# Three sets of turned heads instead of two in the attention of a two-layer diffusion trunk, and the next pair's maxima ahead of the present pair's values

## The chip, the cores and the metric

One core of one Trainium2 chip runs the whole step. The metric is device time in microseconds (us) of one execution. TensorE is called PE in the profile (its weight loads PEld), VectorE DVE, ScalarE ACT, GpSimd POOL; SP issues most DMAs.

## The reference

Two layers with shared structure work on 512 latent tokens and 128 context tokens of width 1024. Each layer is a mixer (a state-space scan, an attention and a gated position mixing side by side, one output projection) and then a gated feed-forward with a short convolution. The change lies in the attention alone, which for the latent tokens is

```python
s = jnp.einsum('bqhd,bkhd->bhqk', q_blk, k).astype(F32) * ATTN_SCALE   # 8 heads, 96 deep
w = jax.nn.softmax(s, axis=-1).astype(v.dtype)                         # 512 queries, 128 + 512 keys
return jnp.einsum('bhqk,bkhd->bqhd', w, v)                             # 64 values a head
```

## The kernel before, in words

The attention of a layer (function `attention`) works on 8 heads in four pairs, p = 0 to 3. Everything is float32; products that need it are made of three matmuls of a high and a low part (qh, ql, kh, kl).

For each head h:
- `turn(h)` (L1223) transposes queries and keys of the head on PE into PSUM (tiles qt and kt, L147) and writes the high parts with ACT (L1229, L1236) and the low parts with DVE (L1230, L1237) into one of **two sets** of tiles, set h % 2. A set is free again when `scores` of the head before in it is done.
- `maxima(h)` (L1241) multiplies each of four blocks of 128 queries with all 640 keys (tile mx, L1248) and takes the negated maximum of each query with DVE (L1250).
- `max_row(h)` (L1254) transposes the four columns of maxima (tile nmt) and copies them with ACT as row 96 into qh (L1259). The row of ones in kh then subtracts the maximum inside the score matmul. `scores(h)` can't begin before it.
- `scores(h)` (L1261) makes five tiles of 128 keys by 512 queries (L1267 to L1269, PSUM tiles s, two slots) and ACT takes the exponential into tiles P (L1271, ten buffers for the ten tiles of a pair).

For each pair, the generator `weighted` (L1275) has two steps: first the sums over the keys' tiles of P (DVE, L1280 and L1282, two buffers Ps) and the **values** (PE, tile o, L1287, both heads side by side); then the **denominators** (PE, L1292) and the copies out of PSUM to yB and S (ACT, `put`, L1208 and L1211).

After pairs 1 and 3 (every two pairs, b = 0 and 1) one DVE reciprocal of 128 x 512 denominators runs (L1427), which two matmuls spread over the partitions (tile rs, L1433 and L1434); yB is scaled by it (L1436) and squared into the sums of a later norm (`squares`, L1350, temporary msq in the pool yb).

In the same stretch PE, SP and ACT do work that has nothing to do with the attention: `fill` is the generator `mod_blocks` (L230), which makes the modulation vectors of the second half of the layer. One step loads 512 KB of w_mod (SP, L258, three buffers raw), multiplies them (PE, tile mod, L261), and after four steps copies (ACT, L267), transposes (PE, modt) and reduces (DVE, L240 to L247). `maxima` gives way after each block of queries, and the caller then takes one step of `fill`. In pair 3 (no next heads) `merge_ac` and the output projection of the two other mixers (L1406 and on, tile wo) run beside the attention.

PSUM tiles: qt, nmt, mod, modt and a few more share two slots (`pz`, L79); kt, mx, o and rs share two slots of two banks (`pb`, L82); s has two slots (`pa`).

What sets the order of the work: the program is written in the order of the Python calls, and when it is built, a planner with a time model of its own issues to each engine, step by step, the earliest written instruction that it takes to be ready and that has its buffers. The written order is thus a ranking; each engine then executes its list in order, and waits at an instruction whose input is late. The loop over the pairs before:

```python
out = weighted(p, [scores(2 * p), scores(2 * p + 1)])
for h in heads:          # 2p + 2 and 2p + 3
    turn(h)
next(out)                # sums and values
for h in heads:
    for _ in maxima(h):
        next(fill, None)
next(out)                # denominators, put
for h in heads:
    max_row(h)
```

Of the kernel before, what the change touches and what calls it, by code (L numbers as in the profile page):

```python
# [11 lines left out]
F32R = mybir.dt.float32r  # L12
# [26 lines left out]
def spans(lo, hi):  # L39
    out = []  # L40
    if lo < 512:
        out.append((lo, min(hi, 512), 0))
    if hi > CX:
        out.append((max(lo, CX), hi, 1))
    return out


class Trunk:
# [1142 lines left out]
    def attention(self, l, M, yb, at, es, qs, ks, Vt, yB, yA, yc, ssc, fill):  # L1191


        nc, V, A = self.nc, self.nc.vector, self.nc.scalar
# [4 lines left out]
        def t(s, sh, dt=F32, bufs=1, pool=at):  # L1199
            return pool.tile(list(sh), dt, name=self.uid(s), tag=s, bufs=bufs)  # L1200

        S = t("S", [128, 2, 640])
        qh, ql, kh, kl = ([t(f"{nm}{i}", [97, n], F32R) for i in range(2)]
                          for nm, n in (("qh", 512), ("ql", 512), ("kh", 640), ("kl", 640)))

        def put(p, ps, sums, n, c):

            A.copy(yB[:, p, c:c + n], ps[:, :n])  # L1208
            r = slice(p % 2 * 64, p % 2 * 64 + 64)
            o = c if c < 512 else 512  # L1210
            A.copy(S[r, p // 2, o:o + n], sums[r, :n])  # L1211

        def constant_rows(i):
            nc.gpsimd.memset(ql[i][96:97].bitcast(F32), 0.0)
            nc.gpsimd.memset(kl[i][96:97].bitcast(F32), 0.0)
            nc.gpsimd.memset(kh[i][96:97].bitcast(F32), 1.0)

        for i in range(2):
            constant_rows(i)

        nml = {}

        def turn(h):  # L1223

            i = h % 2
            ps = self.pz("qt")
            for tt in range(4):
                self.tr(ps[:96, tt * 128:(tt + 1) * 128], qs[:, tt, h, :])
            A.activation(qh[i][:96], ps[:96], AF.Copy, scale=qg)  # L1229
            V.scalar_tensor_tensor(ql[i][:96], ps[:96], qg, qh[i][:96].bitcast(F32),  # L1230
                                   op0=OP.mult, op1=OP.subtract)
            pb = self.pb("kt")
            for kt in range(5):
                self.tr(pb[:96, kt // 4, (kt % 4) * 128:(kt % 4) * 128 + 128], ks[:, kt, h, :])
            for o, a, b in ((0, 0, 512), (1, 512, 640)):
                A.activation(kh[i][:96, a:b], pb[:96, o, :b - a], AF.Copy, scale=kg)  # L1236
                V.scalar_tensor_tensor(kl[i][:96, a:b], pb[:96, o, :b - a], kg,  # L1237
                                       kh[i][:96, a:b].bitcast(F32),
                                       op0=OP.mult, op1=OP.subtract)

        def maxima(h):  # L1241

            i = h % 2
            nm = nml[i] = t("nml", [128, 4], bufs=2)
            for tt in range(4):
                pb = self.pb("mx")
                for o in range(2):
                    mm(pb[:, o, :320], qh[i][:96, tt * 128:(tt + 1) * 128],  # L1248
                       kh[i][:96, o * 320:(o + 1) * 320], start=True, stop=True)
                V.tensor_reduce(nm[:, tt:tt + 1], pb[:, :, :320], axis=AX.XY, op=OP.max,  # L1250
                                negate=True)
                yield

        def max_row(h):  # L1254
            nm = nml[h % 2]
            ps = self.pz("nmt")
            for tt in range(4):
                self.tr(ps[0:1, tt * 128:(tt + 1) * 128], nm[:, tt:tt + 1])
            A.copy(qh[h % 2][96:97], ps[0:1])  # L1259

        def scores(h):  # L1261
            i = h % 2
            Ps = []
            for kt in range(5):
                ps = self.pa("s")
                kc_ = slice(kt * 128, (kt + 1) * 128)
                mm(ps, kh[i][:, kc_], qh[i], start=True, stop=False)  # L1267
                mm(ps, kh[i][:, kc_], ql[i], start=False, stop=False)
                mm(ps, kl[i][:, kc_], qh[i], start=False, stop=True)  # L1269
                P = t("P", [128, 512], bufs=10, pool=at2)  # L1270
                A.activation(P, ps, AF.Exp, scale=SCALE)  # L1271
                Ps.append(P)
            return Ps

        def weighted(p, Ps):  # L1275

            ss = []
            for i in range(2):
                s = t("Ps", [128, 512], bufs=2, pool=at2)
                V.tensor_tensor(s, Ps[i][0], Ps[i][1], op=OP.add)  # L1280
                for kt in range(2, 5):
                    V.tensor_tensor(s, s, Ps[i][kt], op=OP.add)  # L1282
                ss.append(s)
            pb = self.pb("o")
            for kt in range(5):
                for i in range(2):
                    mm(pb[i * 64:(i + 1) * 64, 0], Vt[:, kt, 2 * p + i], Ps[i][kt],  # L1287
                       start=kt == 0, stop=kt == 4)
            yield
            for i in range(2):  # L1290
                r = (2 * p + i) % 4 * 32
                mm(pb[r:r + 32, 1], self.ones[:, :32], ss[i], start=True, stop=True)  # L1292
            put(p, pb[:, 0], pb[:, 1], 512, 0)
            yield


        with self.tc.tile_pool(name=f"actx{l}", bufs=1, side=self.sides[1]) as cx:
            qc, kc = t("qc", [104, 8, 128], pool=cx), t("kc", [104, 8, 128], pool=cx)
            nc.sync.dma_start(out=kc[96:104].rearrange("p h c -> p (h c)"), in_=self.I["k_onehot"])
            for src, dst, g in ((qs[:, 4], qc, qg), (ks[:, 5], kc, kg)):  # L1300
                for hb in range(2):
                    ps = self.pa("ctr")
# [5 lines left out]
            nm = t("nm", [128, 8], pool=cx)  # L1308
            for hb in range(2):
                ps = self.pa("cmx")  # L1310
                for i in range(4):
                    h = 4 * hb + i
# [4 lines left out]
            ps = self.pa("nmt")  # L1317
# [5 lines left out]
            Ps = []  # L1323
            for hb in range(2):
                ps = self.pa("cs")
                for i in range(4):
                    h = 4 * hb + i
                    mm(ps[:, i * 128:(i + 1) * 128], kc[:, h], qc[:, h], start=True, stop=True)
                P = t("Pc", [128, 512], bufs=2, pool=cx)
                A.activation(P, ps, AF.Exp, scale=SCALE)  # L1330
                Ps.append(P)
            for _ in nms[1]:
                next(fill, None)
            for hb, P in enumerate(Ps):
                max_row(hb)
                for p in range(2 * hb, 2 * hb + 2):
                    po = self.pb("co")
                    for i in range(2):
                        h = 2 * p + i
# [7 lines left out]
        at2 = es.enter_context(self.tc.tile_pool(name=f"at2{l}", bufs=1, side=self.sides[1]))  # L1347


        def squares(y, tiles, ac, first):  # L1350
            for a, b, _ in spans(0, NT):
                for i in tiles:
                    if first and i == tiles[0]:
                        A.activation(ac[:, a:b], y[:, i, a:b], AF.Square)
                    else:
                        s = t("msq", [128, 512], pool=yb)
                        A.activation(s[:, :b - a], y[:, i, a:b], AF.Square)
                        V.tensor_tensor(ac[:, a:b], ac[:, a:b], s[:, :b - a], op=OP.add)
# [48 lines left out]
        for p in range(4):  # L1407
            if p == 3:
                yh = M.tile([128, KT, NT], F32R, name=self.uid("yh"), tag="hh", bufs=1)
                yl = M.tile([128, KT, NT], F32R, name=self.uid("yl"), tag="hl", bufs=1)  # L1410
                merge_ac()
                projection = self.project_ac(l, yh, yl)
                next(projection)
            heads = (2 * p + 2, 2 * p + 3) if p < 3 else ()
            out = weighted(p, [scores(2 * p), scores(2 * p + 1)])
            for h in heads:
                turn(h)
            next(out)
            for h in heads:
                for _ in maxima(h):  # L1420
                    next(fill, None)
            next(out)
            for h in heads:
                max_row(h)
            if p % 2:
                b = p // 2
                V.reciprocal(S[:, b, 0:512], S[:, b, 0:512])  # L1427
                if b:
                    for _ in fill:
                        pass  # L1430
                for j in range(2):
                    pb = self.pb("rs")
                    mm(pb[:, 0], self.sel[:, j], S[:, b, 0:512], start=True, stop=True)  # L1433
                    mm(pb[:, 1, :128], self.sel[:, j], S[:, b, 512:640], start=True, stop=True)  # L1434
                    for a, e, c in spans(0, NT):
                        V.tensor_tensor(yB[:, 2 * b + j, a:e], yB[:, 2 * b + j, a:e],  # L1436
                                        pb[:, c, :e - a], op=OP.mult)
                squares(yB, [2 * b, 2 * b + 1], ac, b == 0)
        ps = stats(ac)
# [316 lines left out]
```

## Time and profile before

| | us |
|---|---|
| median of 3 runs (lowest, highest) | 1826.63 (1825.92, 1826.67) |
| the profiled execution | 1826.58 |
| its span, first to last instruction | 1824.8 |
| attention pairs in layer 0, first score to the last reciprocal's use | 272.9 to 394.2 of the span |
| the same in layer 1 | 1153.3 to 1271.5 of the span |

The profile is of one execution; the span leaves out 1.78 us around the first and last instruction. Times in the rows are counted from the span's start. A row of the timeline gives start, length, engine, line, operation and, in brackets, how long the engine stood idle before it and for what. A row of the waits gives the total, the number and the longest of one kind. A stretch (windows) gives per engine the busy time, and PEclk, the share of full speed that TensorE's clock was granted (1.00 is 2.4 GHz, 0.50 is 1.2 GHz).

### The profile page before, as it was taken

The page shows a single profiled execution, that of the slowest core. Times are in us where ns is not written, and L with a number is a line of the kernel's source. Part 1 is how long each engine was busy: PE and PEld are TensorE (multiplying, and loading weights), DVE is VectorE, ACT ScalarE, POOL GpSimd, SP SyncE. Part 2 cuts the span into 40 slices and gives each one's busy share as a digit, 9 for nine tenths or more (in the row PEclk, how much of TensorE's full clock was granted, in tenths as well). Part 3 has the DMA queues.
Part 4 walks back from the last instruction along what each step waited for, and adds up shares of the span by engine and source line. Part 5 has one row for each costly group of instructions (what it writes and reads, how often), then busy time and mean ns, then how long its engine had stood idle before and what let it go on. Part 6 is the DMA issues. An engine that isn't in the chain of part 4 may idle for free.

```text
span 1824.8 us, 28970 instructions
## 1 busy us (share of the span) xinstructions
PE 1694.3 (93%) x11248; PEld 1512.6 (83%) x11248; DVE 1156.8 (63%) x2421; ACT 679.8 (37%) x1210; POOL 312.8 (17%) x738
## 2 busy tenths in 40 slices
PE   5878889999989999999999888999989999999998
PEld 3767755468889999999999876455989999999998
DVE  6887875667674646556477568566786464555564
ACT  4334454433452414224244346343344232332241
POOL 2886200000086060540000120000000000000000
PEclk7889789899899999999999978999989999999999
DMA  9265453301443523234132633540223131331221
GB/s 281 84 174 148 124 162 123 110 15 56 129 137 118 170 56 116 59 94 116 35 90 67 164 105 107 167 133 1 70 70 93 36 104 47 93 92 36 82 82 58
DMA packets 217577, 182.48 MB, mean 100 GB/s; under 512 B 33438, under 2 KB 202204, under 8 KB 217440
## 3 DMA queue, kind: packets, MB, share of 16 engines
q1 hardware_dynamic: 194736, 154.33, 28.2%
q0 software_dynamic: 8272, 23.87, 4.4%
q10 hardware_dynamic: 14432, 2.44, 0.7%
q8 instruction: 89, 1.46, 0.3%
q14 instruction: 48, 0.39, 0.1%
HBM read 161.94 MB, written 18.64 MB: 99 GB/s over the span
## 4 chain that ended last, share of the span: by engine, by line
PE 75%; DVE 10%; DMA 7%; ACT 4%; POOL 2%; issue 2%; ACTq 1%; SPq 0%; DVEq 0%; POOLq 0%
PE up L141 11%; PE up L143 11%; PE up L142 11%; PE dn L142 6%; PE dn L141 6%; PE dn L143 6%; PE o L1287 3%; PE mod L261 2%; DMA raw<-w_mod 2%; PE wo L141 1%; PE wo L143 1%; PE wo L142 1%; DMA raw<-ffn_w_up 1%; PE s L1267 1%; PE win L141 1%
## 5 line engine op out<-in xcount | busy, mean ns | idle before, releaser
L141 PE MATMUL up<-hh,whi 128*128 128x322 f32 x1408 | 435.6, 315 | 8.8 <-ACT hh L357 7.9
L143 PE MATMUL up<-hh,wlo 128*128 128x322 f32 x1408 | 440.9, 314 | 1.1 <-DVE wlo L118 1.0
L142 PE MATMUL up<-hl,whi 128*128 128x322 f32 x1408 | 439.7, 313 | 1.6 <-DVE hl L358 1.5
L141 PEld LDWEIGHTS up<-hh,whi 128*128 128x128 f32 x1408 | 266.1, 191 | 14.3 <-ACT hh L357 7.2
L142 PEld LDWEIGHTS up<-hl,whi 128*128 128x128 f32 x1408 | 268.8, 191 | 2.6 <-DVE hl L358 2.6
L143 PEld LDWEIGHTS up<-hh,wlo 128*128 128x128 f32 x1408 | 267.9, 190 | 2.9 <-DVE wlo L118 1.9
L118 DVE TENSOR_TENSOR wlo<-raw,whi 128x1024 fp32r<-128x1024 f32 (+1 forms) x116 | 146.7, 1266 | 142.2 <-ACT whi L117 141.0
L142 PE MATMUL dn<-glo,dh 128*128 128x322 f32 (+1 forms) x704 | 218.5, 312 | 0.2 <-DVE glo L118 0.2
L143 PE MATMUL dn<-gh,dl 128*128 128x322 f32 (+1 forms) x704 | 217.9, 311 | 0.0
L141 PE MATMUL dn<-gh,dh 128*128 128x322 f32 (+1 forms) x704 | 209.4, 312 | 4.5 <-DVE xT L1501 2.9
L1501 DVE SCALAR_TENSOR_TENSOR xT<-dn,mod,xT 128x320 f32<-128x320 f32 (+2 forms) x288 | 112.2, 435 | 129.5 <-PE dn L143 129.3
L117 ACT CAST whi<-raw 128x1024 fp32r<-128x1024 f32 (+1 forms) x116 | 120.5, 1040 | 151.1 <-PE up L142 56.8
L1532 ACT ACTIVATE cv<-up,prm,cw 128x321 f32<-128x321 f32 x88 | 54.3, 619 | 252.5 <-PE up L143 252.3
L141 PEld LDWEIGHTS dn<-gh,dh 128*128 128x128 f32 x704 | 131.0, 190 | 5.3 <-DVE xT L1501 3.1
L142 PEld LDWEIGHTS dn<-glo,dh 128*128 128x128 f32 x704 | 133.2, 189 | 0.5 <-DVE glo L118 0.5
L143 PEld LDWEIGHTS dn<-gh,dl 128*128 128x128 f32 x704 | 133.5, 190 | 0.0
L1533 DVE SCALAR_TENSOR_TENSOR cv<-up,cw,cv 128x320 f32<-128x320 f32 x88 | 48.3, 549 | 67.5 <-ACT cv L1532 67.5
L261 PE MATMUL mod<-raw,sT 128*32 128x256 f32 x768 | 64.5, 431 | 27.1 <-DMA raw<-w_mod 24.8
L118 DVE TENSOR_TENSOR dl<-raw,dh 128x1024 fp32r<-128x1024 f32 x44 | 54.0, 1227 | 45.8 <-ACT dh L117 45.6
L117 ACT CAST dh<-raw 128x1024 fp32r<-128x1024 f32 x44 | 46.1, 1047 | 56.8 <-DMA raw<-ffn_w_down 50.1
L261 PEld LDWEIGHTS mod<-raw,sT 128*32 128x32 f32 x768 | 19.5, 114 | 57.5 <-DMA raw<-w_mod 29.2
L1250 DVE TENSOR_REDUCE nml<-mx 128x1 f32<-128x640 f32 x64 | 50.9, 820 | 24.0 <-PE mx L1248 23.7
(472 smaller groups left out, 3422.5 us busy)
## 6 DMA issues: line engine op xcount, KB each, us to landing
raw<-w_mod SPq DMA_DIRECT2D x96, 512.0 KB, 4.6
raw<-ffn_w_up SPq DMA_DIRECT2D x88, 512.0 KB, 4.1
raw<-ffn_w_down SPq DMA_DIRECT2D x44, 512.0 KB, 3.5
raw<-w_in SPq DMA_DIRECT2D x10, 512.0 KB, 5.7
we<-WEd POOLq DMA_DIRECT2D x8, 512.0 KB, 4.1
qt<-Qd POOLq DMA_DIRECT2D x8, 512.0 KB, 5.1
raw<-w_out SPq DMA_DIRECT2D x16, 256.0 KB, 5.1
raw<-w_out SPq DMA_DIRECT2D x8, 512.0 KB, 3.4
```

Source lines behind the costliest of these rows:

```text
L117: self.nc.scalar.copy(hi, raw)
L118: self.nc.vector.tensor_tensor(lo, raw, hi.bitcast(F32), op=OP.subtract)
L141: mm(ps, wh, xh, start=start, stop=False)
L142: mm(ps, wh, xl, start=False, stop=False)
L143: mm(ps, wl, xh, start=False, stop=stop)
L261: nc.tensor.matmul(ps[j * 32:j * 32 + 32, c0:c0 + 256], self.sT[:, k0 + j, :], rv[:, j, :], start=k0 == 0, stop=k0 == 4)
L1250: V.tensor_reduce(nm[:, tt:tt + 1], pb[:, :, :320], axis=AX.XY, op=OP.max, negate=True)
L1267: mm(ps, kh[i][:, kc_], qh[i], start=True, stop=False)
L1287: mm(pb[i * 64:(i + 1) * 64, 0], Vt[:, kt, 2 * p + i], Ps[i][kt], start=kt == 0, stop=kt == 4)
L1501: self.nc.vector.scalar_tensor_tensor(self.xT[:, m, a:b], po[:, a - lo:b - lo], self.modcol(l, gi, m, c), self.xT[:, m, a:b], op0=OP.mult, ...
L1532: A.activation(z[:, 0:321], po[:, 0:321], AF.Identity, bias=b, scale=c1)
L1533: V.scalar_tensor_tensor(z[:, 1:321], po[:, 0:320], c0, z[:, 1:321], op0=OP.mult, op1=OP.add)
```

## The change

All in `attention`. There are three sets of turned queries and keys (index h % 3, three nml buffers), so turning a head waits for the scores of the head three before. P has nine buffers instead of ten; of the two sums Ps, the second uses the tile msq of the pool yb, which `squares` uses too. In the loop, each next head is turned, its maxima are taken (with a step of fill each) and its max_row is made, one head after the other, all written ahead of the present pair's sums, values and denominators. The reciprocal of 128 x 512 becomes four of 128 x 128.

```diff
-        qh, ql, kh, kl = ([t(f"{nm}{i}", [97, n], F32R) for i in range(2)]
+        qh, ql, kh, kl = ([t(f"{nm}{i}", [97, n], F32R) for i in range(3)]
...
-        for i in range(2):
+        for i in range(3):
             constant_rows(i)
...
-            i = h % 2
+            i = h % 3
...
-            nm = nml[i] = t("nml", [128, 4], bufs=2)
+            nm = nml[i] = t("nml", [128, 4], bufs=3)
...
-                P = t("P", [128, 512], bufs=10, pool=at2)
+                P = t("P", [128, 512], bufs=9, pool=at2)
...
-                s = t("Ps", [128, 512], bufs=2, pool=at2)
+                s = t("msq", [128, 512], pool=yb) if i else t("Ps", [128, 512], pool=at2)
...
             out = weighted(p, [scores(2 * p), scores(2 * p + 1)])
             for h in heads:
                 turn(h)
-            next(out)
-            for h in heads:
                 for _ in maxima(h):
                     next(fill, None)
+                max_row(h)
             next(out)
-            for h in heads:
-                max_row(h)
+            next(out)
             if p % 2:
                 b = p // 2
-                V.reciprocal(S[:, b, 0:512], S[:, b, 0:512])
+                for c in range(0, 512, 128):
+                    V.reciprocal(S[:, b, c:c + 128], S[:, b, c:c + 128])
```

## Rows read from the trace of the kernel before

**Rows 1.** The page: busy engines of the whole span, and shares of the chain.
```profile
PE 1694.3 (93%) x11248; PEld 1512.6 (83%) x11248; DVE 1156.8 (63%) x2421; ACT 679.8 (37%) x1210; POOL 312.8 (17%) x738
...
PE 75%; DVE 10%; DMA 7%; ACT 4%; POOL 2%; issue 2%; ACTq 1%; SPq 0%; DVEq 0%; POOLq 0%
```

**Rows 2.** Stretches of layer 0's four pairs; cut also at the clock's fall and rise.
```profile
272.92:307.44 34.52, 32.15 (x210) 16.72 (x207) 18.27 (x42) 15.93 (x36) 0.00 (x0) 1.00 0.46 147
307.44:334.79 27.35, 24.64 (x157) 12.49 (x158) 16.47 (x25) 11.44 (x21) 0.00 (x0) 1.00 0.47 145
334.79:344.61 9.82, 9.61 (x29) 6.29 (x30) 6.74 (x9) 3.86 (x5) 0.00 (x0) 0.50 0.59 188
344.61:367.94 23.33, 22.11 (x101) 12.99 (x101) 16.13 (x29) 10.87 (x22) 0.24 (x2) 0.94 0.00 0
367.94:394.23 26.29, 24.34 (x108) 13.68 (x107) 15.64 (x24) 10.60 (x21) 0.00 (x0) 0.98 0.00 1
```

**Rows 3.** The same view of layer 1's low stretch of the clock.
```profile
1215.15:1222.66 7.51, 7.43 (x26) 5.35 (x27) 5.95 (x9) 3.86 (x5) 0.00 (x0) 0.55 0.54 164
```

**Rows 4.** Waits of PE in layer 0's attention: total, times, longest.
```profile
PE mod L261 <- DMA raw<-w_mod: 3.0, 2, 2.1
PE rs L1433 <- DVE S L1427: 1.5, 1, 1.5
PE s L1267 <- ACT qh L1259: 0.8, 3, 0.3
PE mod L261 <- DVE ql L1230: 0.8, 1, 0.8
PE mx L1248 <- DVE nml L1250: 0.7, 2, 0.5
PE mx L1248 <- ACT S L1211: 0.6, 1, 0.6
...
PE nmt L147 <- ACT modev L267: 0.3, 1, 0.3
```

**Rows 5.** Waits of PE in layer 1's attention.
```profile
PE mod L261 <- DMA raw<-w_mod: 4.1, 2, 3.1
...
PE s L1267 <- ACT qh L1259: 0.6, 2, 0.3
...
PE mx L1248 <- DVE nml L1250: 0.5, 1, 0.5
```

**Rows 6.** Timeline of layer 0 between the second and the third pair.
```profile
328.96 3.35 DVE L1427 RECIPROCAL S<-S 128x512 f32<-128x512 f32 x1 [0.27 <-ACT S L1211]
...
333.39 0.64 PE L261 MATMUL mod<-raw,sT 128*32 128x256 f32 x8 [2.13 <-DMA raw<-w_mod]
...
338.15 0.79 PE L1267 MATMUL s<-qh,kh 97*128 97x512 f32 x1 [0.21 <-ACT qh L1259]
```

**Rows 7.** Timeline of layer 1: waits of PE at the same turn and the next.
```profile
1213.76 0.64 PE L261 MATMUL mod<-raw,sT 128*32 128x256 f32 x8 [3.08 <-DMA raw<-w_mod]
...
1215.16 0.54 PE L147 MATMUL nmt<-ident,nml 128*1 128x128 f32 x2 [0.27 <-ACT modev L267]
...
1240.95 0.85 PE L1248 MATMUL mx<-kh,qh 96*128 96x320 f32 x4 [0.59 <-ACT S L1211]
```

**Rows 8.** The tile of the denominators: durations in ns, least, median, most.
```profile
L1346 DVE RECIPROCAL S<-S x4: 952/953/954, 277.1 to 1161.0; 128x128 f32<-128x128 f32 x4
L1427 DVE RECIPROCAL S<-S x4: 3352/3353/3353, 329.0 to 1268.1; 128x512 f32<-128x512 f32 x4
```

**Rows 9.** Timeline of layer 0's first pair: maxima of head 2, then the last values.
```profile
297.31 0.56 PE L1248 MATMUL mx<-kh,qh 96*128 96x320 f32 x2
...
297.81 1.07 PE L1287 MATMUL o<-P,Vt 128*64 128x512 f32 x2
```

**Rows 10.** POOL's timeline: the first of the six memsets of the sets' rows.
```profile
250.67 0.52 POOL L1214 MEMSET ql<- 1x512 f32 x1 [31.83 <-DVE yA L830]
```

**Rows 11.** DVE's group of the maxima in layer 0's attention.
```profile
L1250 DVE TENSOR_REDUCE nml<-mx 128x1 f32<-128x640 f32 x26 | 20.7, 821 | 8.5 <-PE mx L1248 8.3
```

More of the change, by code (lines that the diff above doesn't have):

```diff
@@ L1241, in maxima @@
         def maxima(h):
-            i = h % 2
-            nm = nml[i] = t("nml", [128, 4], bufs=2)
+            i = h % 3
+            nm = nml[i] = t("nml", [128, 4], bufs=3)
             for tt in range(4):
@@ L1254, in max_row @@
         def max_row(h):
-            nm = nml[h % 2]
+            nm = nml[h % 3]
             ps = self.pz("nmt")
@@ L1258, in max_row @@
                 self.tr(ps[0:1, tt * 128:(tt + 1) * 128], nm[:, tt:tt + 1])
-            A.copy(qh[h % 2][96:97], ps[0:1])
+            A.copy(qh[h % 3][96:97], ps[0:1])
         def scores(h):
-            i = h % 2
+            i = h % 3
             Ps = []
```

## The prediction

> **What bounds the kernel now.** The page first: PE is busy 93% of the span and carries 75% of the chain [rows 1]. A change that adds or removes no matmul can win only where PE stands still or runs at a lower clock, so I look for those two, and only in the attention, since nothing else is edited.
>
> The stretches [rows 2, 3] come next: in each pair PE's column nearly fills the stretch. Of layer 0's 121.31 us, PE is idle in 8.5 (121.31 less the five busy times, 112.85). PEclk shows the second loss: 0.50 for 9.82 us in layer 0, 0.55 for 7.51 us in layer 1, both at the turn from the second pair to the third. The work done there would have taken 9.82 x 0.50 = 4.9 us less and 7.51 x 0.45 = 3.4 us less at full clock.
>
> Then who ended PE's waits [rows 4, 5]. The largest are not the attention's own: PE stands at a fill matmul whose load of w_mod hasn't landed, 3.0 us in layer 0 and 4.1 in layer 1, in each layer one of about 1 us and a long one. The long ones, 2.13 and 3.08 us [rows 6, 7], end just before the low clock begins. The waits of the turn from pair to pair are small: scores for the row of maxima, maxima for a reduction, for a PSUM slot that `put` frees, max_row's transposes for a slot behind modev. They come to 0.8 + 0.7 + 0.6 + 0.3 = 2.4 us in layer 0 [rows 4] and 0.6 + 0.5 + 0.6 + 0.3 = 2.0 in layer 1 [rows 5, 7].
>
> At the turn itself [rows 6]: the reciprocal holds DVE for 3.35 us from 328.96 while maxima of heads 4 and 5 still stand behind it; PE waits for the load until 333.39; the first score of the third pair starts at 338.15, right after the row of maxima.
>
> **The change part by part.** I sum against the profiled execution, 1826.58 us (span 1824.8 and 1.78 around it), which is 0.05 under the median of the runs.
>
> *Third set, maxima and max_row ahead of the values.* Number and size of PE's, ACT's and DVE's instructions stay. What moves ahead, per pair: 18 transposes, 8 blocks of maxima with their reductions of 0.82 us [rows 11], 8 steps of fill with their loads on SP, matmuls, modev copies and reductions, and two max_rows. What falls behind: 8 sums on DVE, the values, the denominators, put. SP's queue holds the same loads in the same order; only w_out's loads, which come behind the fill, could move, and they share its three buffers. POOL's queue is not passed. The gain is that a row of maxima is ready while the values, which wait for nothing late, still fill PE, so the small waits of the turn (2.4 + 2.0 = 4.4 us) can go. Their bounds are 0 and 4.4; I take 4.4, because each of them is a wait for a step that would now stand several us earlier. Late next is DVE: the maxima alone are 8 x 0.82 = 6.6 us in a pair, and the sums, whose reading frees P, now stand behind them. DVE is busy 16.47 of 27.35 us in the second pair [rows 2], so it isn't the bound.
>
> *The long waits for the load and the low clock behind them.* They are no wait of the attention, but they fall where the order has nothing but maxima and fill left for PE. With values and next scores at hand, the order can put those in front of a fill matmul whose load is late. If a long wait shrinks to about its short neighbour (0.9 and 1.0: the totals less the longest), layer 0 gains 1.2 us and 4.9 of clock, layer 1 gains 2.1 and 3.4. Bounds: nothing, and all four, 11.6 us. I take one of the two layers: 6.1 or 5.5, 5.8 in the middle. The order is fixed when the kernel is built, by assumed landings, so I can't claim both; the row nearest to such a claim, the same place in both layers, shows the same wait with 1 us of spread.
>
> *Reciprocals in four.* One of 128 x 512 takes 3.353 us, one of 128 x 128 takes 0.953 [rows 8]: four take 3.81, 0.46 more. At the end of pair 3 PE waits 1.5 us for it in each layer [rows 4], so it lies on the path there: 2 x 0.46 = +0.9. The matmul that uses it reads all 512 columns, so no piece lets it start earlier. After pair 1 the pieces let DVE slip other work between them; the maxima are then already ahead, so I count nothing. If that cover is gone, 0.9 more.
>
> *Nine P, one sum in msq.* The tenth exponential of a pair waits until the sum and the values have read the first tile, and behind it in ACT's queue stand copies of the next heads. One fewer buffer can't gain anything. At most it adds one values matmul out of turn, 1.07 us [rows 9], in each of 8 pairs: 8.6. The second sum of pair 2 also waits for the squares of pairs 0 and 1, behind the pieces of the reciprocal, and the P tiles it reads are held so long; pair 3's scores need them only after the merge. I take 0 for both, since PE has other work for 24.64 of 27.35 us in the second pair [rows 2], and keep 8.6 for the upper end.
>
> *Third set of constant rows.* Three more memsets on POOL, an estimate of 1.7 us from the 0.52 of the 512-wide one [rows 10] and two somewhat longer. Needed only by head 2, which is written behind the first scores at 272.92 [rows 2], 22 us later, and POOL idled 31.83 us before them. That wait is for a neighbour's memory; the larger sets reach further into it, which could hold the first turn back by something; nothing taken, 1.7 us if the cover is gone.
>
> Sum: -4.4 - 5.8 + 0.9 = -9.3, so 1817.3. With both layers' waits gone it is -4.4 - 11.6 + 0.9 = -15.1, so 1811.5.
>
> One reading speaks against this. A fill matmul in layer 0 waited 0.8 us for DVE's ql [rows 4], which is the reader of a qt tile: both share the two PSUM slots `pz`, and these stay two. The Trainium skill, Perfetto Trace Analysis, section Optimization Strategy, says that the same gap repeating on the engine that should be saturated can mean there isn't enough SBUF or PSUM for the next tile. By that rule more SBUF sets would leave the gaps of the fill where they are, and the sum would be the second rival's below.
>
> **The rivals.**
> 1. *Forecast: the turn's waits go and the low clock goes in at least one layer.* 1811.5 to 1817.6, 1817.3 taken. For it: the long waits sit where PE has run out of values. Against: a late load, not the attention, ends them.
> 2. *The load decides, and the low clock stays.* Three raw buffers and two `pz` slots are unchanged; so three fill matmuls can go when a slot frees, and the fourth waits for its load. Or the planner had done much of it already: a maxima block of head 2 runs ahead of the last values in the kernel before [rows 9]. Then only the turn's waits go: -4.4 + 0.9 = -3.5, 1823.1.
> 3. *Slower: fill ahead of the values.* The steps of fill now rank above the values, so a fill matmul is issued as soon as its load is assumed there, and PE stands at it with the values queued behind. One more long wait with its low clock per layer costs 2.1 + 4.9 and 3.1 + 3.4, together 13.5; less 3.5 it is +10.0, 1836.6; in one layer only, 1829.8. It decides once a landing lags by as much as the long waits did, behind which the clock fell [rows 2, 6]; a lag of 1 us cost only itself.
>
> **How the numbers follow.** About 0.2%, 3.7 us, is what a measurement of this kernel can tell from no change. Rival 1 has 0.55, rival 2 0.25 (0.03 of it past the bound on the fast side), rival 3 0.20 (0.02 of it within the bound): faster 0.58, same 0.24, slower 0.18. The low end is 1811.5 less the short waits (0.9 + 1.0), the 0.8 for ql and 23.33 x 0.06 = 1.4 us of clock in pair 2 [rows 2]: 1807.4, rounded down to 1807. The high end takes in rival 3 in one layer with a little of the nine P: 1831. The likeliest case's own range is 1807 to 1820 (1817.6 and the 0.9 and 1.7 of the two covers).
>
> **What would show it.** Right: the PEclk of the two turns at 1.00; no wait of s for the row of maxima; no wait of mx for nml or S; the first score of the third pair less than 28 us after that of the second (30.7 now: 307.44 to 338.15); the end's wait for the reciprocal at about 2.0 us. Wrong: waits of mod for w_mod above 3.0 and 4.1 us, a new low stretch of the clock, or P waiting for a buffer with PE idle behind it. The forecast fails if the loads' waits grow by more than the turn's waits shrink.

## The result, and the profile after

The change made the kernel slower: 1838.74 us median of 20 runs (1833.19 to 1844.73) against 1826.65 for the kernel before (20 runs, 1823.51 to 1837.92). The ratio is 1.0062, with a 95% interval of 1.0052 to 1.0072. The forecast was 1817.3, in a range that ended at 1831. The profiled execution took 1838.57 us, with a span of 1836.8.

In the changed kernel the lines from the loop's reciprocal on stand one lower: L1426 is the reciprocal and L1432 the matmul that reads it. The page of after, PE's row and the chain, as in [rows 1]:

```profile
PE 1699.7 (93%) x11248; PEld 1518.0 (83%) x11248; DVE 1159.6 (63%) x2433; ACT 682.7 (37%) x1210; POOL 312.7 (17%) x744
...
PE 34%; DMA 2%; DVE 1%; ACT 1%; issue 0%; ACTq 0%
```

PE is busy 5.4 us longer with the same 11248 instructions. (The chain of after could be followed back over 38% of the span only, so its shares aren't compared.)

The stretches of layer 0's four pairs in after, each from one pair's first score to the next (columns as in [rows 2]), the last to the end of the `rs` matmuls:

```profile
277.26:299.25 21.99, 21.99 (x163) 14.56 (x161) 14.89 (x34) 13.26 (x31) 0.00 (x0) 1.00 0.44 138
299.25:326.62 27.37, 25.73 (x172) 14.23 (x170) 16.10 (x29) 12.27 (x23) 0.00 (x0) 1.00 0.49 154
326.62:358.92 32.30, 28.45 (x120) 15.39 (x118) 22.74 (x37) 15.20 (x26) 0.24 (x2) 0.90 0.30 97
358.92:400.12 41.20, 39.06 (x156) 20.89 (x156) 21.48 (x37) 12.98 (x26) 0.00 (x0) 0.91 0.00 1
```

The turns do come earlier: the first pair's stretch is 12.5 us shorter (34.52 before [rows 2]). But the whole attention, from first score to last `rs`, takes 122.86 us in place of 123.71. What the first pair wins, the later ones give back: the values and denominators of a pair now stand in the next pair's stretch, and the last stretch holds those of two pairs.

PE's waits in after, layer 0 and then layer 1 (total, times, longest), for [rows 4] and [rows 5]:

```profile
PE mod L261 <- DMA raw<-w_mod: 2.6, 3, 1.3
PE mx L1248 <- ACT kh L1236: 2.1, 3, 0.8
PE rs L1432 <- DVE S L1426: 1.6, 1, 1.6
PE mx L1248 <- DVE nml L1250: 0.4, 1, 0.4
...
PE mod L261 <- DMA raw<-w_mod: 3.3, 3, 1.7
PE mx L1248 <- ACT kh L1236: 2.1, 3, 0.8
PE rs L1432 <- DVE S L1426: 1.6, 1, 1.6
```

The waits that were to go have gone or shrunk, and a new one stands in their place, maxima for ACT's `kh`, 2.1 us in each layer. Inside the attention, waits are not where the time went: PE stood idle for 15.8 us of it (both layers), against 17.0 before.

The tile that grew is `o`, the values and denominators. This view counts only `o`, in the attention of layer 0 and of layer 1 (columns: length, PE, PEld and ACT busy on it, PEclk, DMA share, GB/s), first the kernel before, then after:

```profile
272.94:396.65 123.71, 29.48 (x96) 5.92 (x96) 4.46 (x8) 0.94 0.28 88
1153.36:1273.96 120.60, 29.04 (x96) 6.10 (x96) 4.46 (x8) 0.97 0.29 92
```
```profile
277.26:400.12 122.86, 30.31 (x96) 6.89 (x96) 4.47 (x8) 0.94 0.27 85
1159.16:1284.19 125.03, 30.96 (x96) 7.06 (x96) 4.46 (x8) 0.93 0.26 81
```

The same 96 instructions a layer take 58.53 us in before (both layers) and 61.27 in after, 2.7 of the 5.4 us that PE is busy longer.

The second place that changed lies ahead of layer 1's first score. Before the change ACT copied the context's queries at 1125.50; after, it waits for the last of VectorE's query norms. ACT's timeline at that copy, before and after, and then PE's wait behind the same norm in after:

```profile
1125.50 0.68 ACT L1305 ACTIVATE qc<-ctr,qg 96x512 f32<-96x512 f32 x1
```
```profile
1140.16 1.26 ACT L1305 ACTIVATE qc<-ctr,qg 96x512 f32<-96x512 f32 x2 [10.36 <-DVE qs L1189]
...
1140.05 1.94 PE L147 MATMUL qt<-ident,qs 128*96 128x128 f32 x8 [11.28 <-DVE qs L1189]
```

Laid end to end, the 11.99 us by which the profiled execution grew are: attention -0.85 and +4.43, together +3.58; from the first `q` matmul to the first score +2.79 in layer 0 and +6.21 in layer 1, together +9.00; all the rest -0.6. So three quarters of the growth stand ahead of the first scores; in layer 1 it is PE's idle time, 17.8 us of that stretch in place of 9.1.

### The profile page after: what moved, and what is told of

The parts are those of the page before. It is cut to its first block, busy times and chain, and to the rows that moved or that the text cites. A ratio compares the mean times of both kernels' runs of the same rounds, so it can differ in the third digit from the quotient of the medians.

```text
span 1836.8 us, 28967 instructions
## 1 busy us (share of the span) xinstructions
PE 1699.7 (93%) x11248; PEld 1518.0 (83%) x11248; DVE 1159.6 (63%) x2433; ACT 682.7 (37%) x1210; POOL 312.7 (17%) x744
```

## Experiments

Theories: **A**, memory: the larger pool `at` pushes `actx` (the context's `qc`, `kc`, `Pc`) onto the temporaries of the query norms. **B**, the written order itself loses. **C** (from the second group on), nine P under the new order. A2 and A3 name the third set's cost, by place or use, where it is set against C. **D** is the second sum's move into `msq`. Ratios are to the kernel before on the same chip, with their 95% intervals. "Attention" is the sum of both layers' stretches (before 244.31, after 247.89); `o` is PE's time on that tile in them. None of the kernels leaves anything of the computation out. The diffs are shortened to the lines that matter; `...` stands for lines left out.

### Each part alone

**Memory alone.**

```diff
- [t(f"{nm}{i}", [97, n], F32R) for i in range(2)]
+ [t(f"{nm}{i}", [97, n], F32R) for i in range(3)]   # third set laid out, rows written, never read
...
- P = t("P", [128, 512], bufs=10, pool=at2)
+ P = t("P", [128, 512], bufs=9, pool=at2)
...
- s = t("Ps", [128, 512], bufs=2, pool=at2)
+ s = t("msq", [128, 512], pool=yb) if i else t("Ps", [128, 512], pool=at2)
```

> The kernel before with its written order, its two sets in use and its one reciprocal; a third set is only laid out in the pool at (its constant rows written, never read), and the nine P with one s in msq make the room. Theory A (memory: the 9 KB more push the pool of the context's queries and keys, actx, onto the query norms' temporaries, so its transposes wait for the last norm): L1305 qc<-ctr in layer 1 waits some 10 us for VectorE's L1189, the last of the context's scores is 10 to 17 us later than before, and the time is 1831 to 1839. Theory B (the written order loses the time: maxima and fill ahead of the values): no change, 1825 to 1828.

Ratio 1.0005 (0.9991 to 1.0019), 1828.0 us. The wait that A foretold is there, as long as in the changed kernel to the hundredth:

```profile
1133.66 1.26 ACT L1305 ACTIVATE qc<-ctr,qg 96x512 f32<-96x512 f32 x2 [10.36 <-DVE qs L1189]
```

and the time doesn't follow: the kernel is as fast as before. So A explains the wait and not the loss. PE too stood 9.40 us for that norm, but from first `q` to first score layer 1 took only 1.6 us more, 51.70 us (50.13 before).

**The third set elsewhere.** The changed kernel, with the third set in `at2`:

```diff
- [t(f"{nm}{i}", [97, n], F32R) for i in range(3)]
+ [t(f"{nm}{i}", [97, n], F32R) for i in range(2)]
...
+ lst.append(t(f"{nm}2", [97, n], F32R, pool=at2))    # behind the opening of at2
```

> The changed kernel with the third set laid out in at2, which opens after actx is closed, so that actx lies where it lay before; all else as changed. Theory A (memory): the wait of 10 us at L1305 is gone, the context's scores of layer 1 end near 1138 as before, and the time is 1822 to 1830. Theory B (order): 1836 to 1840, as the changed kernel. If both hold in part: 1830 to 1835.

Ratio 1.0046 (1.0023 to 1.0070), 1835.2 us. The wait at L1305 is gone and the attention takes 250.46: most of the loss stays. A falls as the main cause.

**The order alone.** The kernel before, with the loop written as in the change:

```diff
  turn(h)
- next(out)
- for h in heads:
      for _ in maxima(h): next(fill, None)
- next(out)
- for h in heads:
      max_row(h)
+ next(out); next(out)
```

> The kernel before with the new written order alone: two sets, ten P, one reciprocal. Theory A (memory): no loss ahead of the first score; in the attention from nothing to a loss of 4, 1824 to 1831. Theory B (order): 1834 to 1840. By the prediction's own sum without the third set, the turn of the next head would wait for the last score that reads the set, as before, and the gain on the turns would be 2 to 4 us: 1822 to 1825.

Ratio 0.9968 (0.9944 to 0.9992), 1821.6 us: B falls, the order gains. Attention 233.23, and the same view of `o` shows a gain I hadn't counted:

```profile
277.51:394.66 117.15, 24.75 (x96) 6.01 (x96) 4.47 (x8) 0.99 0.30 94
1147.43:1263.51 116.08, 24.75 (x96) 6.02 (x96) 4.46 (x8) 0.99 0.30 95
```

`o` takes 49.5 us, 9.0 less than before.

**The reciprocals alone.**

```diff
- V.reciprocal(S[:, b, 0:512], S[:, b, 0:512])
+ for c in range(0, 512, 128):
+     V.reciprocal(S[:, b, c:c + 128], S[:, b, c:c + 128])
```

> The kernel before with the four reciprocals of 128x128 in place of each 128x512. The prediction took +0.9 for it (four of 0.95 against one of 3.35, twice): 1827 to 1828. Theories A and B: the same, no part of the loss.

Ratio 0.9974 (0.9954 to 0.9994), 1822.5 us: no loss, rather a small gain that I can't place, since its profiled span is 0.2 us from that of before and its attention 245.82.

### Nine P, with and without the new order

**The order with nine P.** To the order alone:

```diff
- P = t("P", [128, 512], bufs=10, pool=at2)
+ P = t("P", [128, 512], bufs=9, pool=at2)
...
- s = t("Ps", [128, 512], bufs=2, pool=at2)
+ s = t("msq", [128, 512], pool=yb) if i else t("Ps", [128, 512], pool=at2)
```

> The kernel of the run with the new order alone (two sets, one reciprocal), with nine P and one s in msq in place of ten and two. Theory C (nine P: the tenth exponential needs one values matmul issued out of turn, ahead of the others, so that values no longer stand in pairs of halves; and ACT holds the key copies behind it, PE waits there and its clock falls): o in layer 1's attention takes about 30 us of PE, as in the changed kernel, where with the order alone it took 24; a low stretch of the clock stands in the last pair; 1830 to 1837. Theory A2 (the third set itself, its memory and its earlier turns, costs the time): as the order alone, 1819 to 1824, o at 24 us.

Ratio 1.0084 (1.0065 to 1.0103), 1841.8 us, above the top of C's range: with no third set at all the kernel is 20 us slower than with ten P. `o` takes 64.0 us:

```profile
274.08:405.05 130.97, 31.32 (x96) 7.01 (x96) 4.46 (x8) 0.93 0.26 83
1161.64:1291.97 130.33, 32.70 (x96) 7.39 (x96) 4.46 (x8) 0.93 0.27 85
```

and exponentials wait for values, which they didn't in before. What ended ACT's idle time before P (total us, times; both layers), in before, with the order alone, and here:

```profile
  PE s L1269: 32.7, 26
```
```profile
  PE s L1269: 22.4, 24
  PE o L1287: 4.5, 2
```
```profile
  PE s L1269: 34.2, 26
  PE o L1287: 6.6, 4
```

The order alone makes them wait nearly as long, so the total is not what sets nine P apart. There it is the first exponential of a pair that waits; here all four are the tenth of a pair, and it is the tenth whose value then comes late. In the changed kernel it is four times the tenth as well, 3.9 us in all.

C expected a low stretch of the clock in the last pair; it stands in layer 0's (0.91) and not in layer 1's (1.00), so that part holds by half.

**Nine P alone.** The same lines on the kernel before:

```diff
- P = t("P", [128, 512], bufs=10, pool=at2)
+ P = t("P", [128, 512], bufs=9, pool=at2)
...
+ s = t("msq", [128, 512], pool=yb) if i else t("Ps", [128, 512], pool=at2)
```

> The kernel before with nine P and one s in msq, nothing else. Theory C: in the order of before the values already stood out of pairs (28 us of o in a layer), so little is lost: 1826 to 1831. Against the run that also laid out the third set (1828.0) it shows the memory's share alone: theory A2 then says 1822 to 1826, theory C the same as that run within 2 us.

Ratio 0.9990 (0.9973 to 1.0007), 1826.2 us. `o` takes exactly what it took:

```profile
sum 246.18, PE 58.53 PEld 12.01 ACT 8.92; mean PE 29.26 PEld 6.01 ACT 4.46
```

In the old order the values stand ahead of the maxima, and no exponential waits for them in this run, so the ninth buffer is enough. The cost belongs to the two edits together. Against the memory run (1.0005) the third set's place comes to 0.15%, inside both intervals.

**Three sets in the old order.** The changed kernel with the loop of before and one reciprocal:

```diff
  turn(h)
+ next(out)
+ for h in heads:
      for _ in maxima(h): next(fill, None)
+ next(out)
+ for h in heads:
      max_row(h)
- next(out); next(out)
...
- for c in range(0, 512, 128):
-     V.reciprocal(S[:, b, c:c + 128], S[:, b, c:c + 128])
+ V.reciprocal(S[:, b, 0:512], S[:, b, 0:512])
```

> The changed kernel with the order of before (turns, values, maxima, denominators, rows of maxima) and one reciprocal: three sets in use, nine P. Theory C: 1826 to 1832, near the run with the third set laid out but unused (1828.0). Theory A2: as the changed kernel, 1833 to 1840. By the prediction, which gave the sets no cost: 1823 to 1828.

Ratio 1.0008 (0.9992 to 1.0025), 1828.3 us, attention 237.24: no loss from using three sets either.

**Order and reciprocals.** The order alone (two sets, ten P), and to it:

```diff
- V.reciprocal(S[:, b, 0:512], S[:, b, 0:512])
+ for c in range(0, 512, 128):
+     V.reciprocal(S[:, b, c:c + 128], S[:, b, c:c + 128])
```

> The new order and the four reciprocals together, with two sets and ten P: the change without what took its room. If both gains add up (1821.6 and 1822.5 alone, against 1827.8): 1814 to 1818. If the four reciprocals only moved the planned order by chance: 1819 to 1824.

Ratio 0.9971 (0.9953 to 0.9989), 1822.9 us: the gains don't add up; the pieces change nothing that can be measured beside the order.

### The buffer given back, and doubled

**The changed kernel with ten P.** Room comes from the first sum, which moves into columns of `qs` that have been turned (in the last pair into `yc`):

```diff
- P = t("P", [128, 512], bufs=9, pool=at2)
+ P = t("P", [128, 512], bufs=10, pool=at2)
...
- t("Ps", [128, 512], pool=at2)
+ qs[:, 0:4, 2*p:2*p + 2].rearrange("p t h d -> p t (h d)")[:, :, 0:128]
```

> The changed kernel (three sets, new order, reciprocals in four) with ten P again; the first head's sum moves out of at2 into columns of qs that have been turned (yc in the last pair), the second stays in msq. Theory C (nine P under the new order): the loss goes, o is back at 24 to 25 us in a layer, 1814 to 1824. Theory A2 (third set, its memory): it stays slower than before by 3 us or more, 1830 to 1840. Between the two if the memory under the query norms costs its 2 to 4 us still: 1820 to 1827.

Ratio 0.9994 (0.9975 to 1.0013), 1827.4 us. One buffer gives back 0.68%, 12.4 us, all of the loss, though not the gain C hoped for. The profiles agree in the attention: 236.50 against 247.89 is 11.4 us less, `o` 50.12 against 61.27 is 11.2 less (the whole profiled executions lie 9.7 apart):

```profile
279.83:398.34 118.51, 25.31 (x96) 6.15 (x96) 4.46 (x8) 0.94 0.27 88
1161.74:1279.73 117.99, 24.81 (x96) 6.01 (x96) 4.46 (x8) 0.94 0.28 87
```

The timelines show how. PE's `o` instructions of layer 0's second pair in after, at full clock (each matmul shows as two instructions):

```profile
331.61 4.50 PE L1287 MATMUL o<-P,Vt 128*64 128x512 f32 x18
...
336.25 1.07 PE L1287 MATMUL o<-P,Vt 128*64 128x512 f32 x2
337.25 1.05 PE L1292 MATMUL o<-Ps,ones 128*32 128x512 f32 x2
...
340.25 1.05 PE L1292 MATMUL o<-msq,ones 128*32 128x512 f32 x2
```

and of the same pair in the run with ten P (L1293 and L1299 are the same two lines):

```profile
332.57 4.51 PE L1293 MATMUL o<-P,Vt 128*64 128x512 f32 x20
337.01 0.62 PE L1299 MATMUL o<-qs,ones 128*32 128x512 f32 x1
337.02 0.62 PE L1299 MATMUL o<-msq,ones 128*32 128x512 f32 x1
337.47 0.59 PE L1299 MATMUL o<-qs,ones 128*32 128x512 f32 x1
337.48 0.59 PE L1299 MATMUL o<-msq,ones 128*32 128x512 f32 x1
```

With ten P, ten values matmuls stand in one row, alternating between the two heads, and the two denominators start 10 ns apart: 4.51 us and 1.06 (337.01 to 338.07), 5.6 in all. In after the tenth tile is late. Nine matmuls take 4.50 us, as long as ten; the tenth follows alone, then the first head's denominator, and 3 us later the second's: 4.50 + 1.07 + 1.05 + 1.05 = 7.7. The heads write different halves of `o` (partitions 0 to 63 and 64 to 127), and neighbours for different halves run beside each other, so a matmul that loses its neighbour is paid in full. Not every pair pays as much: in the first pair of each layer only the tenth value stands alone, and the fourth pair's row is broken up with ten P as well.

Against before, the run with ten P has 7.8 us less in the attention and 8.5 more from first `q` to first score, which the tenth P leaves nearly as it was in after (9.0).

**The same, one reciprocal.**

```diff
- for c in range(0, 512, 128):
-     V.reciprocal(S[:, b, c:c + 128], S[:, b, c:c + 128])
+ V.reciprocal(S[:, b, 0:512], S[:, b, 0:512])
```

> The same with one reciprocal of 128x512. Theory C: within 3 us of the run beside it, 1813 to 1824; if the third set is worth something beyond the new order alone (1821.6), below 1820; if it is not, 1820 to 1824. Theory A2: 1830 to 1838.

Ratio 0.9998 (0.9982 to 1.0013), 1826.5 us, attention 235.93: as the run beside it, and above C's range. The attention has the gain of the order; the whole kernel hasn't.

**The order with ten P and the sum in `msq`.** To the order alone:

```diff
- s = t("Ps", [128, 512], bufs=2, pool=at2)
+ s = t("msq", [128, 512], pool=yb) if i else t("Ps", [128, 512], pool=at2)
```

> The new order with two sets and ten P, the second sum in msq: of the run with nine P (1841.8, 0.84% slower) this leaves only the moved sum. Theory C (the tenth P): 1819 to 1825, as the new order alone. Rival D (msq, which the squares of the merge and of yB use too, holds the second sum back, and with it P): 1833 to 1842.

Ratio 0.9961 (0.9944 to 0.9979), 1820.5 us. Rival D falls: it is the number of P and not the moved sum.

**Eight P.**

```diff
- P = t("P", [128, 512], bufs=9, pool=at2)
+ P = t("P", [128, 512], bufs=8, pool=at2)
```

> The new order with two sets and eight P, the second sum in msq: the suspected shortage doubled. Theory C: two exponentials of each pair wait for values out of turn, 1846 to 1865. If the loss is a step that the first missing tile brings whole: 1838 to 1846. Rival D: 1838 to 1846 as well.

Ratio 1.0103 (1.0086 to 1.0120), 1845.6 us, just below the range that C gave for two tiles and within that of a step: the intervals of eight and nine P meet. The first missing tile brings nearly the whole loss, since one late tile of the second head already parts values and denominators. The second adds little: at full clock the values of a pair then stand in rows of 3.65, 1.08 and 1.07 us, in place of 4.50 and 1.07.

### What the missing tile costs by, and where the third set lies

**Values by head.** The order alone, ten P, neighbours broken up on purpose:

```diff
- for kt in range(5):
-     for i in range(2):
+ for i in range(2):
+     for kt in range(5):
          mm(pb[i * 64:(i + 1) * 64, 0], Vt[:, kt, 2 * p + i], Ps[i][kt], ...)
```

> The new order alone (two sets, ten P), with the values' loop turned round: five tiles of the first head, then five of the second, so that matmuls into the two halves of o no longer alternate. Theory C says that two neighbours into different halves run beside each other (0.27 us each in a long alternating row, 0.54 alone), and that the nine P broke such neighbours up: o rises from 24 to some 40 to 45 us in a layer and the time by 30 to 40 us, 1850 to 1862. If neighbours don't matter and only the wait for P does: no change, 1819 to 1824.

Ratio 1.0107 (1.0081 to 1.0133), 1846.9 us, 25 above the order alone. `o` takes 75.8 us in place of 49.5, and the row of the second pair, at full clock, 7.14 in place of 4.51:

```profile
274.48:409.50 135.02, 37.96 (x96) 9.92 (x96) 4.47 (x8) 0.94 0.25 80
1159.18:1293.67 134.49, 37.83 (x96) 9.91 (x96) 4.47 (x8) 0.94 0.26 82
...
334.05 7.14 PE L1287 MATMUL o<-P,Vt 128*64 128x512 f32 x20
```

The mechanism is C's, at about seven tenths of the price I expected: 37.9 us of `o` in a layer, not 40 to 45. The trace shows why. Read by the written order, where the first head ends and the second begins (336.68 to 338.02), the last two matmuls of the one and the first two of the other still run side by side, their instructions starting at most 0.06 us apart; the other twelve instructions follow each other at 0.43 us. So partners needn't stand directly side by side, and the row takes less than ten matmuls one by one. No P is short here, so the order of the matmuls alone can cost more than the whole loss. It isn't `o` alone: against the order alone the attention is 36.3 us longer (269.51), with a granted clock of 0.94 in place of 0.99, and the rest of the profiled execution 11.5 shorter, which no run explains.

**Third set in `at2`, ten P, one reciprocal.** To the run with three sets, ten P and one reciprocal:

```diff
- [t(f"{nm}{i}", [97, n], F32R) for i in range(3)]
+ [t(f"{nm}{i}", [97, n], F32R) for i in range(2)]
...
+ lst.append(t(f"{nm}2", [97, n], F32R, pool=at2))
```

> Three sets, the new order, ten P (first sum in turned columns of qs), one reciprocal, with the third set laid out in at2 so that actx lies where it lay before. Theory A3 (what is left of the third set's cost is its place under the context's queries and keys, some 5 us ahead of the first score of layer 1): that goes, 1818 to 1823, at or below the two sets in the same order. If the third set costs by its use (earlier turns that draw DVE and ACT away from the running pair): as with three sets in at, 1825 to 1829.

Ratio 0.9938 (0.9919 to 0.9957), 1817.8 us: faster than both kernels, about 10 us under before and, by the ratios, 1.2% under the changed kernel. Attention 235.36; the copy of `qc` no longer waits for the norms, and the last pair of layer 0 runs at full clock (its stretch of the pair view):

```profile
354.47:391.88 37.41, 36.02 (x166) 20.22 (x166) 20.55 (x35) 12.02 (x25) 0.12 (x1) 1.00 0.00 1
...
1120.19 0.68 ACT L1313 ACTIVATE qc<-ctr,qg 96x512 f32<-96x512 f32 x1
```

From first `q` to first score it takes 59.60 and 49.57 us, against 60.90 and 53.92 in the run with the set in `at`, 5.7 us less. The ratios of the two lie 0.6% or 11 us apart, but the two profiled executions only 3.5 (1821.20 and 1817.66), so the profiles can't show where the 11 us come from.

**Two sets, the third laid out; and its control without it.** To the run with three sets, ten P and one reciprocal (the set in `at`), first the index (and with it the `nml` buffers, two again), then also the layout:

```diff
- i = h % 3
+ i = h % 2
...
- [t(f"{nm}{i}", [97, n], F32R) for i in range(3)]      # the control only
+ [t(f"{nm}{i}", [97, n], F32R) for i in range(2)]
```

> The new order with two sets in use, ten P and one reciprocal, the sums as in the run beside it; the third set laid out in at and never read. Theory A3 (place alone): 1824 to 1829, first score of layer 1 some 52 to 56 us after the first q matmul (50 before). If it is the use of the third set: 1818 to 1823.

> The same with the third set not laid out: the control for both. Both theories: as the new order alone, 1817 to 1823. If the sum in the columns of qs costs something itself: 1824 to 1828, and the runs beside it carry that as well.

Ratios 1.0009 (0.9991 to 1.0026) and 1.0003 (0.9983 to 1.0023), 1831.1 and 1828.3 us. The first lies above A3's range, with 51.96 us from first `q` to first score in layer 1. The control missed what both theories said of it, and its time is at the top of what the third case gave for a cost of the moved sums. But its attention is as short as any (235.15), and the best run has the moved sums too. What is long is layer 1 from first `q` to first score, 56.94 us, though `actx` isn't displaced: in this build the last `q` matmul ends 21.2 us behind the first, against 14.9 in before. So this pair can't price the place. The order is planned anew in every build, and stretches that no edit touched differ by several us between these traces (one execution of each kernel): layer 0's FFN, from first to last `up`, takes 479.5 to 488.8 us.

The late `q` matmuls stand in after too (22.2 us), in both runs with ten P and the set in `at` (21.0 and 19.8), and in two kernels with nothing in that place (20.1 with the set in `at2`, 20.4 with two sets and nine P). So the place doesn't make them, and layer 1's +6.21 isn't the place's alone. Where the last `q` came early (14.9 to 15.6), layer 1 took 51.70 to 53.92 us to the first score with the set in `at` (three runs) and 48.10 to 51.27 without it (nine kernels, before among them): about 3 us between the means, an estimate. In layer 0 the same stretch takes 57.48 to 62.63 us without a third set, so its +2.79 can't be put down to the set at all.

## Why the prediction was wrong

**The step that failed** is "Nine P, one sum in msq": "I take 0 for both, since PE has other work", with 8.6 as the upper end. It measured 12.4 us by the ratios (after against after with ten P), 11.4 in the attention's stretches; 21.4 lie between the forecast and the result. The step saw that the tenth exponential would wait for the first tile's readers, and asked who would cover PE's wait; in the attention PE indeed hardly waits (the longest new wait is 0.8 us). The cost isn't a wait: it is PE's own busy time. The price of one matmul out of turn, 1.07 us [rows 9], was read from the right row, but charged once a pair, and only in the upper end. A late tile parts the second head from the first, and PE pays for what the parted values and denominators had shared, 2.1 us in the pair shown. "Number and size of PE's, ACT's and DVE's instructions stay" held for PE; I took from it that PE's busy time couldn't change.

The rule for this is in the Trainium skill, TensorE: Matmul & The Clock Gate, Part 3: Packing small matmuls — row/col tiling: matmuls at different tile positions of the array run concurrently. The traces agree: ten matmuls for two halves take 4.51 us, nine 4.50. Neither the prediction nor its bound used it.

**Short waits of the turn, -4.4.** Named rightly: `s` for the row of maxima, `mx` for S are gone, `mx` for `nml` shrank to 0.4. "Late next is DVE" was wrong: late next is ACT, with 2.1 us of `mx` for `kh` in each layer. These 4.2 us take back nearly all of the 4.4. The sign that I gave for the turn came true in layer 0, with 27.37 us from the second pair's first score to the third's: it told of that turn and not of the time. The reading that spoke against, the fill's 0.8 us for `ql`, is not among after's waits.

**Long waits and low clock, -5.8.** The long waits shrank, from 2.1 and 3.1 to 1.3 and 1.7 us, and the low clock at the turn to the third pair went: layer 0's second stretch has PEclk 1.00 where [rows 2] had 9.82 us at 0.50 (layer 1's has 0.94). But a new low stretch stands in the two later ones: 32.30 x 0.10 + 41.20 x 0.09 = 6.9 us lost at the lower level of 1.2 GHz, as much as before (4.9 + 23.33 x 0.06 + 26.29 x 0.02 = 6.8). The tenth P leaves it there (0.92 and 0.89), so it is no part of the 12.4 us. With the order alone the attention's mean clock is 0.99 in both layers.

**A gain that wasn't in the sum.** The order let the planner set all ten values of a pair in one row, in the first three pairs of each layer: `o` went from 58.5 to 49.5 us. In before, the rows stood broken up, which [rows 9] showed: a lone pair of instructions at 1.07 us.

**Reciprocals, +0.9.** The wait at the end grew from 1.5 to 1.6 us in each layer, not 2.0 ([rows 4] show the 1.5 for layer 0 alone; layer 1 has the same), and no run with the pieces was slower than its neighbour without by more than the intervals.

**Third set of constant rows, 0.** I named the reach into the neighbour's memory and took nothing. The wait of 10.36 us is shown to come from the place: it is there with the set laid out and unused, and gone with the set in `at2`. Its price isn't settled: 0.15% by the memory run against nine P alone, 0.16% by moving the set in the changed kernel, nothing by the last pair, 0.6% by the best run. Only that run stands clear of its neighbour by the intervals, and it also has its last `q` matmul early (15.0 us, against 19.8). The 9.0 us ahead of the first scores, which with the 12.4 come to the size of the miss, are thus explained in part only: about 3 us by the place in layer 1, an estimate; the late `q` matmuls and layer 0's share stay open.

**The rivals.** Rival 2 kept the low clock where it was; it moved instead. Rival 3 had the sign and nearly the time (1836.6), by the wrong mechanism: no long wait for a load was added, and fill ahead of the values gains by itself. The forecast's size, 1817.3, is what the change gives with the tenth P, one reciprocal and the set out of the way (1817.8), which is luck in part: a gain that wasn't in its sum stands in for terms that came only in part.

## What to carry to other kernels

When a change takes one buffer from a ring to make room, ask which two instructions stood side by side because that tile was ready, not only who waits. An edit that costs nothing in one order can cost the most in another: test pairs of edits, not only each alone. And compare PE's busy time by tile first when the instruction count is the same; here that one view named the cause, while the waits pointed elsewhere.

## What the runs showed of the hardware

Matmuls that fill 64 partitions each, for different halves of the partitions, run beside each other when they stand close together in PE's queue: a row of ten that alternates takes 4.51 us, nine of it 4.50, the same ten head by head 7.14, all at full clock. In the last, two matmuls of each head still overlap where the heads meet; a lone one costs 1.07. Writing all pairs head by head cost 25 us of 1821 here, and the order of two loops was the only edit.
